# A state-space layer in fp32 on one core: D times x moved to ScalarE, decays issued earlier, the z projection ordered bank by bank

## The chip, the cores and the metric

One core of a Trainium2 chip runs the whole program. Time is device time in microseconds (us) of one execution. The engines are named as the profile names them: PE (TensorE, matmuls), DVE (VectorE), ACT (ScalarE), POOL (GpSimd) and SP (SyncE, which issues most DMAs). L followed by a number is a line of the kernel before; line numbers above 1020 differ a little in the kernel after.

## What is computed

Two request groups, a prompt of 256 tokens and eight samples of 16 tokens, 384 tokens in all, go through two layers of width 1024. The first layer is a short convolution beside forgetting attention, the second a Mamba-2 mixer; a gated convolutional FFN follows each. Everything is fp32. The change is in the second mixer, which is, cut to what matters:

```
def odd_mixer(h, conv_state, ssm_state, w_in, conv_w, conv_b, dt_bias, a_log, d_skip, norm_w, w_out):
    proj = h @ w_in
    z, xbc, dt_raw = jnp.split(proj, [D_INNER, D_INNER + CONV_DIM], axis=-1)
    xbc, new_conv = causal_dwconv(xbc, conv_state, conv_w, conv_b)
    xbc = jax.nn.silu(xbc)
    xs, bm, cm = jnp.split(xbc, [D_INNER, D_INNER + SSM_GROUPS * D_STATE], axis=-1)
    dt = jax.nn.softplus(dt_raw.astype(f32) + dt_bias.astype(f32))
    a = -jnp.exp(a_log.astype(f32))
    ...
    y, h_last = ssd_scan(xs, dt, a, bm, cm, ssm_state, chunk)
    y = y + d_skip.astype(f32)[:, None] * xs.astype(f32)
    y = y.reshape(b, length, D_INNER) * jax.nn.silu(z.astype(f32))
    y = rms_norm(y.reshape(b, length, SSM_GROUPS, D_INNER // SSM_GROUPS), ...)
    out = y.astype(h.dtype) @ w_out
```

There are four groups of eight heads, 64 wide each, so a group is 512 of the 2048 inner channels. Inside a group the scan is done by matrices: decay factors between tokens times C·B ("mix") times x gives the part within a block, the incoming state gives the part between blocks, and the states are carried on.

## The kernel before

Each large product is three matmuls (function three, L418 on): the weights and the activations are split into a high and a low part, and high times high, high times low and low times high are summed. A weight tile is 128 x 1024. It comes by one DMA of 512 KB into raw, ACT copies it to wh (L306) and DVE subtracts to get wl (L300). Three buffers each of raw, wh and wl exist; Weights.take (L385) makes the next tile ahead at high priority as soon as the current one is first used. Weights of the output projection also carry the norm's gain; such a tile is made in four pieces on ACT and four on DVE. The order in which tiles come is fixed on the host by the list that the diff's first piece changes.

In this layer PE keeps the program order (keep, L220 on); the order on the other engines comes from the Tile scheduler, which follows the program and the priorities, the work marked high priority first. PSUM is split into three banks "mm" (for the channel products xbc, the z projection and the output projection op) and five "aux" banks for all else. A bank is written again only after its reader has emptied it.

One group g goes like this:

- conv_bc and conv_x project channels: B and C are one product each of 24 matmuls of 128 x 384, and x is four products. After each product, DVE copies it to pad (times the row norm R), three DVE instructions and one of ACT do the convolution c, ACT applies silu to xf, B or C.
- turn_x (L1006) transposes the four x tiles on PE and ACT copies them to xt. Group.take (L1051) makes xdt on DVE and xw on POOL. Group.skip (L1067) makes y = D·x, on POOL, three instructions of 128 x 512, and loads the samples' states h0.
- decays (L1019) loads four tiles td from a DRAM copy of the running sums, ACT does relu in 16 instructions and exp in four (with table loads between), and Group (L1037) multiplies td by C·B on DVE.
- within (L1079) runs on PE: S, the prompt block's own state, and y from mix and xdt; inter (L1103) is yi, the part from the incoming state, for which ACT copies S to S0; states (L1119) is hn, the samples' new states, in two halves.
- project_z (L1132) is 72 matmuls of 128 x 512 into three banks (z0, z1, z2, one for each 128 tokens), from four weight tiles; Gate multiplies y by silu(z), takes the squares, builds the norm's factor rg by a chain of small DVE instructions (rqi to rqo) and turns y for the output projection add_out (L1193), which is 96 matmuls of 128 x 384 for a group, each of its eight outputs (op) added into X by DVE.

The main loop (L1264 to L1303) runs groups 0 to 2 and places within(g), yi, the next group's channel products, hn, z(g) and half or all of op(g-1) in that order. The last group (L1305 to L1321) has the same steps without new channel products. sgS is a single product ahead of the loop whose exponential decS gives the samples' decays. In the rows of the trace, tiles carry a running number that differs between the two kernels (y__5139, td__4920).

The lines around the first group, before:

```
    ps = paux("sgS")
    T.matmul(ps, lhsT=C("Us"), rhs=tjd.rearrange("p h j -> p (h j)"), start=True, stop=True)
    act(decS, ps, AF.Exp)

    decs = decays(0)
    grp = Group(0, decs, bc_)
    Bn, Cn = conv_bc(0, 1), conv_bc(1, 1)
    nx = [conv_x(1, 0)]
    grp.take(turn_x(xs))
    grp.skip()
    xs = [*nx, conv_x(1, 1)]
```

## Time and profile before

| | |
|---|---|
| median of 3 runs | 1072.57 us (1071.39 to 1074.22) |
| the profiled execution | 1072.5 us, of which the traced span is 1070.5 |
| PE busy | 1039.9 us, 97% of the span |
| DVE busy | 747.5 us, 70% |
| ACT busy | 503.9 us, 47% |
| POOL busy | 133.6 us, 12% |

The state-space mixer is on PE from about 466 to 790 us of the span. The attention layer with its FFN stands before it, the second FFN behind it. Shares of busy time are means over the whole span. What PE waits for in the mixer's stretch, and which engine is full there, is read from that stretch alone.

### The profile page before, as it was taken

The page shows a single profiled execution, that of the slowest core. Times are in us where ns is not written, and L with a number is a line of the kernel's source. Part 1 is how long each engine was busy: PE and PEld are TensorE (multiplying, and loading weights), DVE is VectorE, ACT ScalarE, POOL GpSimd, SP SyncE. Part 2 cuts the span into 40 slices and gives each one's busy share as a digit, 9 for nine tenths or more (in the row PEclk, how much of TensorE's full clock was granted, in tenths as well). Part 3 has the DMA queues.
Part 4 walks back from the last instruction along what each step waited for, and adds up shares of the span by engine and source line. Part 5 has one row for each costly group of instructions (what it writes and reads, how often), then busy time and mean ns, then how long its engine had stood idle before and what let it go on. Part 6 is the DMA issues. An engine that isn't in the chain of part 4 may idle for free.

```text
span 1070.5 us, 16702 instructions
## 1 busy us (share of the span) xinstructions
PE 1039.9 (97%) x6316; PEld 968.5 (90%) x6316; DVE 747.5 (70%) x1361; ACT 503.9 (47%) x825; POOL 133.6 (12%) x351
## 2 busy tenths in 40 slices
PE   9999999999999999999699999899999999999998
PEld 7788799999999999988577877797999999999998
DVE  7968566777776634467898978977997776765332
ACT  6344335444444433347666755663554444443221
POOL 0030010100000000013433223320001000000000
PEclk9999999999999999998899999999999999999999
DMA  8442434443434444436446463643534434344441
GB/s 286 156 148 76 159 120 125 126 131 121 135 119 136 128 128 128 125 104 189 127 137 214 144 235 128 208 144 105 178 121 127 134 120 136 119 131 140 138 148 43
DMA packets 50328, 150.30 MB, mean 140 GB/s; under 512 B 5992, under 2 KB 8312, under 8 KB 50248
## 3 DMA queue, kind: packets, MB, share of 16 engines
q1 hardware_dynamic: 44360, 136.78, 41.0%
q10 hardware_dynamic: 4608, 8.39, 2.1%
q0 software_dynamic: 1280, 4.06, 1.1%
q8 instruction: 50, 0.82, 0.3%
q14 instruction: 30, 0.25, 0.1%
HBM read 135.81 MB, written 13.40 MB: 139 GB/s over the span
## 4 chain that ended last, share of the span: by engine, by line
PE 34%; DVE 14%; ACT 4%; issue 2%; DMA 1%; ACTq 0%; POOL 0%; DVEq 0%
PE fd L240 9%; PE fg L240 9%; PE fa L240 8%; PE z L240 4%; DVE c L303 3%; DVE wl L300 2%; PE xbc L240 2%; DVE wl L303 1%; ACT wh L306 1%; DVE X L300 1%; PE y L240 1%; DVE pad L300 1%; DMA raw<-w 1%; PE op L240 1%; ACT L306 1%
## 5 line engine op out<-in xcount | busy, mean ns | idle before, releaser
L300 DVE TENSOR_TENSOR wl<-raw,wh 128x1024 fp32r<-128x1024 f32 (+1 forms) x205 | 252.2, 1231 | 140.4 <-ACT wh L306 139.9
L306 ACT ACTIVATE wh<-raw 128x1024 fp32r<-128x1024 f32 (+1 forms) x205 | 216.1, 1055 | 224.0 <-PE fd L240 95.0
L240 PE MATMUL fg<-Hh,wh 128*128 128x384 f32 x352 | 118.4, 336 | 1.0 <-DVE pad L300 1.0
L240 PE MATMUL fa<-Hl,wh 128*128 128x384 f32 x352 | 118.7, 337 | 0.4 <-DVE Hl L303 0.4
L240 PE MATMUL fg<-Hl,wh 128*128 128x384 f32 x352 | 118.6, 337 | 0.0
L240 PE MATMUL fa<-Hh,wl 128*128 128x384 f32 x352 | 118.4, 336 | 0.0
L240 PE MATMUL fg<-Hh,wl 128*128 128x384 f32 x352 | 118.4, 336 | 0.0
L240 PE MATMUL fa<-Hh,wh 128*128 128x384 f32 x352 | 118.3, 336 | 0.0
L240 PE MATMUL fd<-hh,wh 128*128 128x384 f32 x352 | 118.3, 336 | 0.0
L240 PE MATMUL fd<-hh,wl 128*128 128x384 f32 x352 | 118.3, 336 | 0.0
L240 PE MATMUL fd<-hl,wh 128*128 128x384 f32 x352 | 118.3, 336 | 0.0
L303 DVE SCALAR_TENSOR_TENSOR c<-pad,prm,c 128x400 f32<-128x400 f32 (+1 forms) x160 | 104.8, 658 | 7.0 <-ACT c L306 5.3
L240 PE MATMUL xbc<-Hh,wh 128*128 128x384 f32 x192 | 67.6, 352 | 2.1 <-DVE X L300 2.1
L240 PEld LDWEIGHTS fg<-Hh,wh 128*128 128x128 f32 x352 | 66.2, 188 | 1.3 <-ACT R L306 1.3
L240 PEld LDWEIGHTS fa<-Hl,wh 128*128 128x128 f32 x352 | 66.2, 188 | 1.0 <-DVE Hl L303 0.8
L240 PEld LDWEIGHTS fa<-Hh,wl 128*128 128x128 f32 x352 | 66.2, 188 | 0.1
L240 PEld LDWEIGHTS fg<-Hh,wl 128*128 128x128 f32 x352 | 66.2, 188 | 0.1
L240 PEld LDWEIGHTS fg<-Hl,wh 128*128 128x128 f32 x352 | 66.2, 188 | 0.1
L240 PEld LDWEIGHTS fa<-Hh,wh 128*128 128x128 f32 x352 | 66.2, 188 | 0.1
L240 PEld LDWEIGHTS fd<-hl,wh 128*128 128x128 f32 x352 | 66.2, 188 | 0.0
L240 PEld LDWEIGHTS fd<-hh,wh 128*128 128x128 f32 x352 | 66.2, 188 | 0.0
L240 PEld LDWEIGHTS fd<-hh,wl 128*128 128x128 f32 x352 | 66.2, 188 | 0.0
(803 smaller groups left out, 2140.6 us busy)
## 6 DMA issues: line engine op xcount, KB each, us to landing
raw<-w SPq DMA_DIRECT2D x219, 512.0 KB, 3.5
kc<-kc SPq DMA_DIRECT2D x8, 256.0 KB, 3.6
vc<-vc SPq DMA_DIRECT2D x8, 256.0 KB, 3.1
X<-x SPq DMA_DIRECT2D x8, 192.0 KB, 3.8
o_y<-X SPq DMA_DIRECT2D x8, 192.0 KB, 2.7
o_v<-vt POOLq DMA_DIRECT2D x3, 256.0 KB, 2.5
o_k<-kraw POOLq DMA_DIRECT2D x3, 256.0 KB, 2.6
cst<-cst SPq DMA_DIRECT2D x1, 617.0 KB, 4.8
```

The lines of the kernel that those rows point to most:

```text
L240: ins = nc.tensor.matmul(*a, **kw)
L300: (eng or V).tensor_tensor(out=out, in0=a, in1=b, op=op)
L303: V.scalar_tensor_tensor(out=out, in0=a, scalar=s, in1=b, op0=op0, op1=op1)
L306: S.activation(out, a, f, **kw)
```

## The change

- **D·x.** Three POOL instructions for each group become eight ACT instructions (Copy with a scale by head, 128 x 3 x 64 each) into one y tile for three blocks, two buffers. The late output projection's scratch o takes a buffer of xdt instead of one of y.
- **First decays.** decays is a generator in two parts: the DMAs of td first, the ACT work later. For group 0 the DMAs are issued ahead of the products bc(0,1), bc(1,1) and x(1,0), which now stand ahead of sgS; then turn_x, the ACT part of the decays, Group, take, and x(1,1) and x(1,2) stand ahead of the first y.
- **S0** is copied at high priority.
- **z.** Instead of pairs of weight tiles with banks 0 and 1 and then bank 2, project_z takes half of the contraction (four takes, two weight tiles) and runs it bank by bank, 12 matmuls each. In group 0 a third of z now stands ahead of hn's first half, a third between the halves, and a third behind.
- **Output half.** In group 2, 48 matmuls of op stand behind the last channel product and ahead of hn's second half and the third z; the weights' order and the gain positions follow.

```diff
--- before.py
+++ after.py
@@ -132,7 +132,7 @@

     bc(0, 0), bc(1, 0), xs(0), bc(0, 1), bc(1, 1), xs(1), tm(wi, 0)
     bc(0, 2), bc(1, 2), xs(2, (0, 1)), out(0, (0, 256)), xs(2, (2, 3)), tm(wi, 512), out(0, (512, 768))
-    bc(0, 3), bc(1, 3), xs(3), tm(wi, 1024), out(1), tm(wi, 1536), out(2), out(3)
+    bc(0, 3), bc(1, 3), xs(3), out(1, (0, 256)), tm(wi, 1024), out(1, (512, 768)), tm(wi, 1536), out(2), out(3)
     ffn(1)
     w = np.concatenate(blocks, 1)
     a["w"] = w.reshape(P, -1, RC).transpose(1, 0, 2)
@@ -353,7 +353,7 @@
             self.tiles, self.made, self.raw, self.pos = {}, 0, None, 0

             t, self.gain = 32 + 3 * NF + 8, {}
-            for g, at in enumerate(((12, 13, 20, 21), range(32, 36), range(40, 44), range(44, 48))):
+            for g, at in enumerate(((12, 13, 20, 21), (28, 29, 34, 35), range(40, 44), range(44, 48))):
                 self.gain.update({t + i: 4 * g for i in at})
             self.total = d["w"].shape[0] * (RC // WC)

@@ -1021,13 +1021,16 @@
         out = []
         for b in range(2):
             for hf in range(2):
-                c0 = 8 * g + 4 * hf
                 dec = t512("td", 4, (P, 4, P))
-                nc.sync.dma_start(out=dec, in_=rows[b, c0:c0 + 4, :].partition_broadcast(P))
+                nc.sync.dma_start(out=dec, in_=rows[b, 8 * g + 4 * hf:8 * g + 4 * hf + 4, :].partition_broadcast(P))
+                out.append(dec)
+        yield
+        for b in range(2):
+            for hf in range(2):
+                c0, dec = 8 * g + 4 * hf, out[2 * b + hf]

                 for i in range(4):
                     act(dec[:, i, :], dec[:, i, :], AF.Relu, scale=-1.0, bias=cumK[:, 32 * b + c0 + i:32 * b + c0 + i + 1])
-                out.append(dec)
         for dec in out:
             act(dec, dec, AF.Exp, scale=-1.0)
         return out
@@ -1071,10 +1074,11 @@
                 h0 = t512("h0", 8)
                 nc.sync.dma_start(out=h0, in_=d["h0"][bb, self.g])
                 self.h0.append(h0)
-            for b in range(3):
-                y = t512("y", 6)
-                tt(heads(y[:, :]), heads(self.xt[:, b, :]), bc64(prr("dsk", 32)[:, self.h8]), ALU.mult, G)
-                self.ys.append(y)
+            y = t512("y", 2, (P, 3, 512))
+            for h in range(8):
+                o = slice(64 * h, 64 * h + 64)
+                act(y[:, :, o], self.xt[:, :, o], AF.Copy, scale=prc("dsk", 8 * self.g + h))
+            self.ys = [y[:, b, :] for b in range(3)]

         def within(self):

@@ -1085,7 +1089,8 @@
                     T.matmul(ph, lhsT=self.Bt[:, b, :], rhs=self.xw[b], start=True, stop=True)
                     if b == 0:
                         self.S0 = t512("S0", 1)
-                        act(self.S0, ph, AF.Copy)
+                        with tc.high_priority():
+                            act(self.S0, ph, AF.Copy)
                     else:
                         S1 = self.xt[:, 0, :]
                         tt(heads(S1), heads(self.S0[:, :]), bc64(E[:, 224 + 8 * g:232 + 8 * g]), ALU.mult)
@@ -1132,14 +1137,13 @@
     def project_z():

         ps = [pmm(f"z{b}") for b in range(3)]
-        for k0 in range(0, KT, 2):
-            ws = [W.take(512) for _ in range(2)]
-            for bs in ((0, 1), (2,)):
+        for k0 in (0, 4):
+            ws = [W.take(512) for _ in range(4)]
+            for b in range(3):
+                o = slice(b * P, (b + 1) * P)
                 for i, (wh, wl) in enumerate(ws):
-                    for b in bs:
-                        o = slice(b * P, (b + 1) * P)
-                        three(ps[b], Hh[:, k0 + i, o], Hl[:, k0 + i, o], wh, wl, k0 + i == 0, k0 + i == KT - 1)
-                        yield
+                    three(ps[b], Hh[:, k0 + i, o], Hl[:, k0 + i, o], wh, wl, k0 + i == 0, k0 + i == KT - 1)
+                    yield
         zs = t512("zs", 1, (P, 3, 512))
         for b in range(3):
             act(zs[:, b, :], ps[b], AF.Silu, scale=r[:, b:b + 1])
@@ -1203,7 +1207,7 @@
                 if factor is None:
                     residual(m0 + m, ps)
                 else:
-                    o = t512("y", 6, (P, NT))
+                    o = t512("xdt", 3, (P, NT))
                     tt(o, ps[:, :NT], factor, ALU.mult)
                     tt(X[:, m0 + m, :], X[:, m0 + m, :], o, ALU.add)
                     norm_tile(m0 + m, "g_ffn", 1, o1)
@@ -1246,6 +1250,10 @@
     cumK = o0.tile([P, 64], F32, name="cumK")
     V.tensor_copy(cumK, ps[:, 0:64])
     tt(wdt, E[:, 96:192], dt, ALU.mult)
+    decs = decays(0)
+    next(decs)
+    Bn, Cn = conv_bc(0, 1), conv_bc(1, 1)
+    nx = [conv_x(1, 0)]
     tjd = t512("h0", 8, (P, 32, LB))
     tt(tjd, dA[:, 64:96].unsqueeze(2).broadcast_to([P, 32, LB]),
        C("Tj").unsqueeze(1).broadcast_to([P, 32, LB]), ALU.mult)
@@ -1253,13 +1261,11 @@
     T.matmul(ps, lhsT=C("Us"), rhs=tjd.rearrange("p h j -> p (h j)"), start=True, stop=True)
     act(decS, ps, AF.Exp)

-    decs = decays(0)
-    grp = Group(0, decs, bc_)
-    Bn, Cn = conv_bc(0, 1), conv_bc(1, 1)
-    nx = [conv_x(1, 0)]
-    grp.take(turn_x(xs))
+    xt = turn_x(xs)
+    grp = Group(0, run(decs), bc_)
+    grp.take(xt)
+    xs = [*nx, conv_x(1, 1), conv_x(1, 2)]
     grp.skip()
-    xs = [*nx, conv_x(1, 1)]
     op = gate = None
     for g in range(4):
         last = g == 3
@@ -1271,20 +1277,24 @@
             op = add_out(*gate.y2, None)
         if last:
             break
-        decs = decays(g + 1)
+        decs = run(decays(g + 1))
         xs.append(conv_x(g + 1, len(xs)))
         grp.inter(1)
         bc_ = turn_bc(g + 1, Bn, Cn)
-        if g == 1:
+        z = project_z()
+        if g == 0:
+            steps(z, 8)
+        elif g == 1:
             steps(op, 16)
         else:
-            xs.append(conv_x(g + 1, len(xs)))
+            xs.append(conv_x(3, 1))
         grp.states(0)
-        z = project_z()
         if g == 0:
-            steps(z, 12)
+            steps(z, 8)
         while len(xs) < 4:
             xs.append(conv_x(g + 1, len(xs)))
+        if g == 2:
+            steps(op, 16)
         grp.states(1)
         nxt = Group(g + 1, decs, bc_)
         zs = steps(z)
```

In the following lists, one row is one instruction, or a run of equal ones (x4), in the order of its engine's stream.

ACT, first group, ahead of the first y. Before, from the first exponential of td to the copy of S (td__4920 is what the first y needs; xt is the transposed x; wh are weight tiles for later products):

```order
L306 ACTIVATE td__4920<-td__4920 128x512
L306 ACTIVATE wh_5297<-raw_5295 128x1024
L306 ACTIVATE td__4926<-td__4926 128x512
L306 ACTIVATE td__4932<-td__4932 128x512
L306 ACTIVATE td__4938<-td__4938 128x512
L306 ACTIVATE c4_4993<-pad4_4986,prm_74 128x408
L306 ACTIVATE c4_5039<-pad4_5032,prm_74 128x408
L306 ACTIVATE xt__5092<-xT_5093 128x512
L306 ACTIVATE xt__5092<-xT_5099 128x512
L306 ACTIVATE xt__5092<-xT_5105 128x512
L306 ACTIVATE wh_5365<-raw_5363 128x1024
L306 ACTIVATE S0__5193<-S_5191 128x512
```

After, the same stretch up to the first exponential of td (td__4915 is now what the first y needs):

```order
L306 ACTIVATE wh_5346<-raw_5344 128x1024
L306 ACTIVATE td__4919<-td__4919,cumK_4912 128x128 x4
L306 ACTIVATE td__4921<-td__4921,cumK_4912 128x128 x3
L306 ACT_TABLE_LOAD
L306 ACTIVATE xf__5015<-c4_5054 128x256
L306 ACTIVATE wh_5415<-raw_5413 128x1024
L306 ACTIVATE S0__5242<-S_5240 128x512
L306 ACTIVATE xf__5015<-c4_5054 128x128
L306 ACTIVATE td__4921<-td__4921,cumK_4912 128x128
L306 ACT_TABLE_LOAD
L306 ACTIVATE td__4915<-td__4915 128x512
```

The exponentials, which stood ahead of xt and of S0, now stand behind S0 and a second table load, with two weight copies ahead of them.

DVE, first group. Before, ending with the first xdt (c4 and pad4 are convolutions, xdt__5111 the operand of the first y):

```order
L303 SCALAR_TENSOR_TENSOR c4_4993<-pad4_4986,prm_74,c4_4993 128x408
L303 SCALAR_TENSOR_TENSOR c4_5039<-pad4_5032,prm_74,c4_5039 128x408
L303 SCALAR_TENSOR_TENSOR c4_4993<-pad4_4986,prm_74,c4_4993 128x408
L303 SCALAR_TENSOR_TENSOR c4_5039<-pad4_5032,prm_74,c4_5039 128x408
L303 SCALAR_TENSOR_TENSOR c4_4993<-pad4_4986,prm_74,c4_4993 128x408
L300 TENSOR_TENSOR wl_5366<-raw_5363,wh_5365 128x1024
L303 SCALAR_TENSOR_TENSOR c4_5039<-pad4_5032,prm_74,c4_5039 128x408
L300 TENSOR_TENSOR pad4_5078<-xbc_5047,R_79 128x256
L300 TENSOR_TENSOR pad4_5078<-xbc_5047,R_79 128x8x16
L300 TENSOR_TENSOR xdt__5111<-xt__5092,dt_4535 128x512
L300 TENSOR_TENSOR xdt__5115<-xt__5092,dt_4535 128x512
L303 SCALAR_TENSOR_TENSOR c4_5085<-pad4_5078,prm_74,c4_5085 128x408
```

After, ending with the four td:

```order
L300 TENSOR_TENSOR wl_5347<-raw_5344,wh_5346 128x1024
L303 SCALAR_TENSOR_TENSOR c4_5054<-pad4_5047,prm_74,c4_5054 128x408
L300 TENSOR_TENSOR xdt__5119<-xt__5066,dt_4535 128x512
L300 TENSOR_TENSOR pad4_5155<-xbc_5124,R_79 128x256
L300 TENSOR_TENSOR pad4_5155<-xbc_5124,R_79 128x8x16
L300 TENSOR_TENSOR pad4_5201<-xbc_5170,R_79 128x256
L300 TENSOR_TENSOR pad4_5201<-xbc_5170,R_79 128x8x16
L300 TENSOR_TENSOR wl_5416<-raw_5413,wh_5415 128x1024
L300 TENSOR_TENSOR td__4915<-td__4915,CB__4833 128x512
L300 TENSOR_TENSOR td__4917<-td__4917,CB__4833 128x512
L300 TENSOR_TENSOR td__4919<-td__4919,CB__4833 128x512
L300 TENSOR_TENSOR td__4921<-td__4921,CB__4833 128x512
```

xdt stood behind two products' convolutions. Now it stands ahead of the pads of the next ones, and td comes last, behind a weight tile's wl.

DVE, group 2, around the start of the third z. Before (pad4_6891 empties the bank of the last channel product, h0 are the samples' states, wl_7009 is the first gain tile):

```order
L300 TENSOR_TENSOR pad4_6891<-xbc_6860,R_79 128x256
L303 SCALAR_TENSOR_TENSOR c4_6852<-pad4_6845,prm_74,c4_6852 128x408
L300 TENSOR_TENSOR pad4_6891<-xbc_6860,R_79 128x8x16
L300 TENSOR_TENSOR h0__6536<-h0__6536,hn_6905 128x512
L300 TENSOR_TENSOR h0__6540<-h0__6540,hn_6906 128x512
L303 SCALAR_TENSOR_TENSOR c4_6898<-pad4_6891,prm_74,c4_6898 128x408
L300 TENSOR_TENSOR h0__6544<-h0__6544,hn_6907 128x512
L303 SCALAR_TENSOR_TENSOR c4_6898<-pad4_6891,prm_74,c4_6898 128x408
L300 TENSOR_TENSOR h0__6548<-h0__6548,hn_6908 128x512
L303 SCALAR_TENSOR_TENSOR c4_6898<-pad4_6891,prm_74,c4_6898 128x408
L300 TENSOR_TENSOR wl_6985<-raw_6982,wh_6984 128x1024
L303 SCALAR_TENSOR_TENSOR wl_7009<-raw_7006,prm_74,wh_7008 128x256 x4
```

After (op_6932 is the first output of the op half; X is the residual):

```order
L300 TENSOR_TENSOR mix__7017<-CB__6742,decS_4539 128x1024
L300 TENSOR_TENSOR wl_6963<-raw_6960,wh_6962 128x1024
L303 SCALAR_TENSOR_TENSOR c4_6861<-pad4_6854,prm_74,c4_6861 128x408
L303 SCALAR_TENSOR_TENSOR c4_6913<-pad4_6906,prm_74,c4_6913 128x408
L303 SCALAR_TENSOR_TENSOR c4_6861<-pad4_6854,prm_74,c4_6861 128x408
L303 SCALAR_TENSOR_TENSOR c4_6913<-pad4_6906,prm_74,c4_6913 128x408
L300 TENSOR_TENSOR wl_7025<-raw_7022,wh_7024 128x1024
L303 SCALAR_TENSOR_TENSOR c4_6861<-pad4_6854,prm_74,c4_6861 128x408
L303 SCALAR_TENSOR_TENSOR c4_6913<-pad4_6906,prm_74,c4_6913 128x408
L300 TENSOR_TENSOR X_73<-X_73,op_6932 128x384
L300 TENSOR_TENSOR X_73<-X_73,op_6946 128x384
L300 TENSOR_TENSOR X_73<-X_73,op_6966 128x384
```

The convolutions of the last two x products and two wl now stand ahead of the first addition that empties an op bank, and the gain tiles have moved further up, out of these rows.

## Rows read from the trace of the kernel before

**Rows 1.** What PE waited for between 466 and 805 us, by what it waited for: us in total, times, longest.

```profile
PE y L240 <- DVE xdt__5111 L300: 7.9, 1, 7.9
PE z L240 <- DVE pad L300: 3.7, 2, 3.4
PE sgS L240 <- DVE h__4915 L300: 2.4, 1, 2.4
PE xbc L240 <- DVE X L300: 1.4, 1, 1.4
PE yi L240 <- ACT S__5785 L306: 1.3, 1, 1.3
```

**Rows 2.** Windows of all engines: from:to, length, busy us (instructions) of PE, PEld, DVE, ACT and POOL, granted TensorE clock, DMA share, GB/s.

```profile
490.00:500.00 10.00, 7.56 (x34) 5.67 (x33) 8.88 (x17) 9.78 (x14) 4.17 (x9) 0.76 0.59 185
500.00:510.00 10.00, 10.00 (x54) 10.00 (x53) 3.33 (x6) 6.58 (x19) 0.78 (x4) 0.90 0.87 272
...
520.00:530.00 10.00, 2.95 (x34) 2.32 (x34) 10.00 (x13) 3.06 (x6) 8.07 (x12) 0.63 0.22 67
...
656.70:694.90 38.20, 34.62 (x243) 28.08 (x242) 37.59 (x62) 26.26 (x53) 14.70 (x21) 0.96 0.58 190
```

**Rows 3.** Timeline of PE around the first group: start us, us, engine, line, operation, out<-in, count, and in brackets the wait before it.

```profile
495.82 2.07 PE L240 MATMUL sgS<-h__4915,cst 128*128 128x512 f32 x2 [2.44 <-DVE h__4915 L300]
...
512.17 0.27 PE L245 MATMUL xT<-cst,xf__4691 128*128 128x128 f32 x1
...
518.04 1.13 PE L240 MATMUL S<-xw__5113,Bt__4840 128*128 128x512 f32 x2 [0.22 <-POOL xw__5113 L300]
...
527.05 0.38 PE L240 MATMUL y<-xdt__5111,td__4920 128*64 128x64 f32 x2 [7.88 <-DVE xdt__5111 L300]
```

**Rows 4.** Timeline of PE, second group: the start of its first channel product and of what follows 72 matmuls later.

```profile
567.03 0.42 PE L240 MATMUL xbc<-Hh,wh 128*128 128x384 f32 x1
...
579.61 1.02 PE L240 MATMUL S<-xw__5613,Bt__5354 128*128 128x512 f32 x2
```

**Rows 5.** Timeline of ACT, first group: one td tile's relu, the table load behind it, the first exponential.

```profile
509.30 1.26 ACT L306 ACTIVATE td__4938<-td__4938,cumK 128x128 f32<-128x128 f32 x4
510.59 1.28 ACT L306 ACT_TABLE_LOAD   x1
511.88 0.63 ACT L306 ACTIVATE td__4920<-td__4920 128x512 f32<-128x512 f32 x1
```

**Rows 6.** Timeline of DVE, first group, up to the operand of the first y.

```profile
516.45 6.00 DVE L303 SCALAR_TENSOR_TENSOR c<-pad,prm,c 128x408 f32<-128x408 f32 x5
522.37 2.06 DVE L300 TENSOR_TENSOR wl<-raw,wh 128x1024 fp32r<-128x1024 f32 x1
...
526.23 0.68 DVE L300 TENSOR_TENSOR xdt__5111<-xt__5092,dt 128x512 f32<-128x512 f32 x1
```

**Rows 7.** Windows with the instructions of tile z alone (columns as in Rows 2, engines that have none left out): the two halves of the first z, then the second and the third z whole.

```profile
547.00:556.20 9.20, 8.82 (x36) 6.61 (x36) 0.00 (x0) 1.00 0.45 153
557.30:565.80 8.50, 8.50 (x36) 6.68 (x36) 1.38 (x2) 1.00 0.96 308
...
616.00:633.50 17.50, 17.18 (x72) 13.36 (x72) 1.38 (x2) 1.00 0.81 277
683.80:705.70 21.90, 18.48 (x72) 14.37 (x72) 1.38 (x2) 0.92 0.82 268
```

**Rows 8.** Timeline of ACT: a weight copy in the first z, and the last gain copies and the copy of S in group 1.

```profile
562.15 1.06 ACT L306 ACTIVATE wh<-raw 128x1024 fp32r<-128x1024 f32 x1 [4.75 <-DMA raw<-w]
...
583.83 1.69 ACT L306 ACTIVATE wh<-raw,prm 128x256 fp32r<-128x256 f32 x4
585.42 0.57 ACT L306 ACTIVATE S__5785<-S 128x512 f32<-128x512 f32 x1
```

**Rows 9.** Timeline of POOL, group 1: one D·x.

```profile
572.84 1.56 POOL L300 TENSOR_TENSOR y__5779<-xt__5565,prm 128x512 f32<-128x512 f32 x1
```

**Rows 10.** Timeline of DVE, group 1: two instructions of the chain to rg, of 128 x 3 elements each.

```profile
571.93 0.97 DVE L311 TENSOR_SCALAR rqi<-v 128x3 int32<-128x3 int32 x1
...
575.46 0.16 DVE L303 SCALAR_TENSOR_TENSOR rqb<-rqa,v 128x3 f32<-128x3 f32 x1
```

**Rows 11.** Timeline of PE: half of op(0) and two channel products (to S of group 2), and the whole op(1) (to S of group 3).

```profile
634.72 0.42 PE L240 MATMUL op<-yh,wh 128*128 128x384 f32 x1
...
654.03 1.02 PE L240 MATMUL S<-xw__6357,Bt__5973 128*128 128x512 f32 x2
...
706.91 0.42 PE L240 MATMUL op<-yh,wh 128*128 128x384 f32 x1
...
724.23 0.59 PE L240 MATMUL S<-xw__7097,Bt__6740 128*128 128x512 f32 x1
```

**Rows 12.** Timeline of DVE, group 2: the pads of x(3,0), then later a convolution step, a wl, a gain tile's wl, and an addition into X.

```profile
668.75 0.61 DVE L300 TENSOR_TENSOR pad<-xbc,R 128x256 f32<-128x256 f32 x2
...
693.56 0.64 DVE L303 SCALAR_TENSOR_TENSOR c<-pad,prm,c 128x408 f32<-128x408 f32 x1
694.32 1.23 DVE L300 TENSOR_TENSOR wl<-raw,wh 128x1024 fp32r<-128x1024 f32 x1
698.02 1.68 DVE L303 SCALAR_TENSOR_TENSOR wl<-raw,prm,wh 128x256 fp32r<-128x256 f32 x4 [2.48 <-ACT wh L306]
...
709.90 0.55 DVE L300 TENSOR_TENSOR X<-X,op 128x384 f32<-128x384 f32 x1
```

## The prediction

> **What bounds the kernel now.** PE is busy for 97% of the span, so only PE's stream counts: where it waits, and where its clock is down. I read the waits of PE in the mixer's stretch first [rows 1]. There are 16.7 us in five of them: the first y (7.9), the third z (3.4 of 3.7), sgS (2.4), the products behind the first op half (1.4) and the second group's yi (1.3). The windows come next [rows 2]. The granted clock is 0.76, 0.90 and 0.63 in the windows in and behind the waits of sgS and y, where PE stood idle, so PE runs part of them at the lower of its two levels, and a wait removed can give back more than its own length. Third is what ends each wait: PE's timeline [rows 3], then ACT [rows 5] and DVE [rows 6] behind it. The reader is to see that the first y waits for DVE, which at that point works off two products' convolutions, and that DVE is full around the third z (37.59 of 38.2 us) [rows 2]. The sum is made against the profiled execution, 1072.5 us, 0.07 below the median.
>
> **sgS: -5.1.** Before, sgS starts at 495.82 after 2.44 idle, and 72 xbc matmuls later the transposes start at 512.17 [rows 3]: 16.35 us. At the full clock those 72 take 12.58 [rows 4]; the first of sgS's two passes shown as one row and their issue take about 1.06, half of that row's 2.07. So 16.35 - 13.64 = 2.7 went to the low clock. Now 72 products stand where PE waited; h__4915 is long done when PE gets to sgS. Gain 2.44 + 2.7 = 5.1. Bounds: 2.4, if the clock falls anyway, and 5.1.
>
> **First y: -3.0.** With that, sgS runs at about 506 and S of the first block starts at about 517, behind 24 products more than before. The y behind it needs td, and td now has a longer way on ACT: relu (1.26 a tile), a table load (1.28), xf, a weight copy (1.06), S0 (0.57), the rest of a relu, another table load, one exponential (0.63), then DVE's product (0.68) [rows 5, 6, 8]. From S's end at 518.1: S0 to 518.9, the small ones to 519.7, the load to 521.0, the exponential to 521.6, DVE to 522.4, and about 0.6 for the weight tile's wl ahead of it: 523.0. PE waits 5 there against 8.1 (7.88 and 0.22 [rows 3]), so -3.0. Bounds: 0 (it waits 8 again: a DMA or a conv queue in front of td) and -7 (ACT gets ahead of S0). The 24 products moved ahead are work either way. The low clock behind the wait [rows 2] I keep at its cost of before.
>
> **First z: +1.5.** Bank by bank, two weight tiles must stay until bank 2 has used them. The fourth tile's buffers come free at matmul 30 of 72 and are needed at matmul 43: 13 matmuls at 8.50 / 36 = 0.236 [rows 7] cover 3.07 us. Its wh (1.06 [rows 8]) and wl (1.23 [rows 12]) take 2.3, plus about 0.4 of handing over: covered on idle engines. But DVE's queue holds mix, td and the h additions in that stretch, of which I put four (0.68 each [rows 6]) in front: 5.3 - 3.07 = 2.2 of waiting. The first half lost 0.7 before (9.2 against 8.5 [rows 7]). Net +1.5; bounds -0.7 and +4.
>
> **Second group: -2.0.** POOL's D·x ran beside DVE's small chain to rg, whose 128 x 3 instructions took 0.97 there and 0.16 beside idle POOL [rows 9, 10]; four such cost about 3.3 us of rg. The eight new ACT instructions are bounded by the 0.31 that a 128-element relu adds in a row of four (1.26 / 4) and by the 0.57 of a 128 x 512 copy [rows 5, 8]; 192 elements lie near the lower end, 0.34 each, 2.75 a group. rg therefore comes 3.3 earlier and ACT is 2.75 later: half a microsecond ahead, and S0 also passes one of four gain pieces (1.69 / 4 = 0.4 [rows 8]). That takes 0.9 of yi's 1.3 wait [rows 1]; the two waits of yT behind it lose about the same 1.1 together, since DVE's additions of y no longer stand behind the stretched chain. Bounds -2.4 and +1 (at 0.57 each, ACT is 4.6 later and S0 1.3 late).
>
> The Trainium skill, "SBUF — State Buffer", section "Who interferes with whom", says that a DVE instruction with two SBUF inputs contends with a GpSimd operation that reads SBUF, and that one of them blocks for the whole instruction. By that, all of the 1.5 us of each D·x beside DVE would come back, also under the 6.00 us of five convolution steps; the trace agrees as far as two-input steps go, but rqi, with one input, was slow as well. Taking it whole would give the larger gain that is the first rival below.
>
> Speaking against the change, the Trainium skill, "ScalarE: Activation LUTs", section "Rules for kernel authors", wants multiplications on VectorE and not on ScalarE. By the costs in its section "What ACT_TABLE_LOAD costs", an estimate for 192 elements with one pointer operand is 0.35 us back to back, 2.8 a group. No row here has this form; 2.8 would leave the sum as it is.
>
> **Second z: +0.4.** The same tile boundary with a less loaded DVE: I take 0.9 of waiting, less the 0.5 that this z loses now (17.5 against 2 x 8.5 [rows 7]). Bounds -0.5 and +3.
>
> **First op half: -2.2.** From op to S it takes 19.31 us [rows 11]. Full-clock pieces give 48 op at 17.32 / 96 [rows 11] = 8.66 and 48 xbc at 12.58 x 48 / 72 [rows 4] = 8.39, together 17.05. The missing 2.2 are X additions late on a DVE that POOL held up, the 1.4 of [rows 1] among them. I take it all back; bounds 0 and -2.3.
>
> **Third z and the new op half: +1.6.** Before, this z lost 21.9 - 17.0 = 4.9 [rows 7]: 3.4 of waiting for the last pad, which empties the third bank, and 1.5 of clock. Now 48 op stand between. Three banks: the fourth output needs the first X addition, which stands on DVE behind all convolutions. From the pads at 668.75 [rows 12] to it there are 12 convolution steps (0.64), 3 wl (1.23), 2 gain tiles (1.68), 12 additions and td (0.68), mix (as a wl, 1.23), 4 pads (0.61), CB (0.6) and the addition (0.55) [rows 6, 12]: 27.7, less 0.08 of overlap at each of some 40 [rows 6]: 24.5. That is 693.5 to 694, where PE wants the bank at about 682.8 + 36 x 0.18 = 689.3. So 4.5 to 5 of waiting, and 1.5 of clock behind it: 6.5 against 4.9. Bounds: +4, and -4.5 where DVE, rid of POOL, is early.
>
> **The rest: 0.** The fourth z, the late add_out's scratch, and the DMA issues of decays on SP, moved ahead of three products whose raw loads they precede by four issues, are covered by PE's work. Bounds 0 and +0.5.
>
> Sum: -5.1 - 3.0 + 1.5 - 2.0 + 0.4 - 2.2 + 1.6 = -8.8, so 1063.7 us.
>
> **The rivals.**
> *DVE is freed further.* If each of four groups loses some 4.5 us of POOL's D·x beside DVE (3 x 1.5 [rows 9]), the backlog in front of the third z is gone: no boundary waits in the z's (first -0.7, second -0.5) and -4.5 at the third: -5.1 - 3.0 - 0.7 - 2.4 - 0.5 - 2.2 - 4.5 = -18.4, 1054 us; I take 1056, as the chain of convolutions itself stays. For it: rqi's 0.97 against 0.16 for its like. Against it: DVE is paced by products that come no faster.
> *The first y waits as before.* The way over ACT has two table loads; one more weight copy or a late DMA keeps 8: the sum is -5.8, and with boundary waits of 1 us more, 1067.7. Against it: the row sum ends 4 us early.
> *The z's starve: slower.* Every half boundary has to wait for a tile whose raw comes late; one weight copy waited 4.75 us for its DMA [rows 8], beside a DMA share of 0.96 [rows 7]. If in all four z the fourth tile is ready 3.5 us late, with 1.5 of clock behind it, that is 20, against 12.3 of other gains: 1080 us. It decides from the point where raw lands less than 2.7 us before matmul 43. Against it: three raws are held ahead.
> *DVE paces all.* It is 37.59 of 38.2 full [rows 2]; if PE's gains are only waited for later, the time stays at 1071. Against it: the waits of sgS and the first y lie ahead of that stretch, and windows behind the third z are not full.
>
> **How the numbers follow.** Chances: forecast 0.53 (1060 to 1067), DVE freed 0.15, first y as before 0.15, DVE paces all 0.09, starving 0.08. The range leaves out the last two: 1054.5 to 1069. A measurement tells 0.3% (3.2 us): faster is below 1069.4, which holds the first three, but for 0.02 of the third: 0.81; same: 0.09 + 0.02 = 0.11; slower 0.08.
>
> **What would show it.** In the profile after: no wait of sgS and a clock of 1.0 there; a first y at about 523 with a wait near 5, released by td; in the first z one wait of about 2 at its middle, by a wl; small DVE instructions of 0.16 throughout; an op in group 2 that waits 4 to 5 for X. A first y at 527 or later, waits at several half boundaries, or no wait at op's fourth output would make the sum wrong at that term.

## The result and the profile after

The changed kernel took 1062.71 us (median of 4 runs, 1061.36 to 1065.19) against 1072.91 (1071.39 to 1074.22) before: a ratio of 0.9908, 95% interval 0.9885 to 0.9931. On a second chip it was 1063.06 against 1069.46, 0.9931 (0.9914 to 0.9948). The forecast, 1063.7, is 0.9918 of the 1072.5 us it was summed against. The profiled execution of after is the slowest of its four, 1065.19 us with a span of 1063.4.

The same view as [rows 1], what PE waited for in the mixer, of the changed kernel:

```profile
PE y L240 <- DVE td__4915 L300: 4.6, 1, 4.6
PE op L240 <- DVE X L300: 3.8, 1, 3.8
PE z L240 <- DVE wl L300: 1.6, 2, 0.9
PE z L240 <- ACT wh L306: 1.0, 2, 0.7
...
PE z L240 <- DVE pad L300: 0.5, 1, 0.5
PE op L240 <- DVE pad L300: 0.5, 1, 0.5
```

The waits of sgS, of yi and of the third z are gone. The first y still waits, now for td; two waits are new, in the z's (wl and wh) and at op's fourth output (X). The windows of all engines that answer to [rows 2]:

```profile
490.00:500.00 10.00, 10.00 (x64) 9.50 (x63) 8.71 (x19) 7.65 (x11) 3.69 (x8) 1.00 0.53 155
500.00:510.00 10.00, 10.00 (x61) 9.47 (x60) 8.34 (x15) 8.17 (x18) 3.12 (x13) 1.00 0.90 312
...
520.00:530.00 10.00, 7.29 (x114) 4.62 (x114) 8.45 (x15) 9.95 (x21) 2.34 (x7) 0.83 0.48 150
...
680.00:690.00 10.00, 8.25 (x34) 5.75 (x35) 6.37 (x12) 2.23 (x5) 0.00 (x0) 0.83 0.37 106
```

The granted clock is 1.00 where it was 0.76 and 0.90; it is down only in the windows of the two long waits that are left. PE's timeline around the first group, to be read beside [rows 3]:

```profile
506.56 0.59 PE L240 MATMUL sgS<-h__5061,cst 128*128 128x512 f32 x1
...
507.42 0.27 PE L245 MATMUL xT<-cst,xf__4691 128*128 128x128 f32 x1
...
517.06 0.59 PE L240 MATMUL S<-xw__5113,Bt__4840 128*128 128x512 f32 x1
...
522.71 0.34 PE L240 MATMUL y<-xdt__5111,td__4915 128*64 128x64 f32 x2 [4.63 <-DVE td__4915 L300]
```

The stages on PE, in us from one first matmul to the next, in two profiles of each kernel ("again" is e9 and e1 below; "term" is the prediction's). Stages that are equal are left out.

| stage | before | after | before, again | after, again | change by pair | term |
|---|---|---|---|---|---|---|
| first xbc to the transposes | 52.12 | 46.51 | 51.66 | 46.51 | -5.6, -5.2 | -5.1 |
| to the first y, 24 xbc (4.17) more | 14.88 | 15.29 | 14.88 | 15.29 | -3.8, -3.8 | -3.0 |
| to the first z, 24 xbc and a hn (1.07) less | 20.02 | 13.62 | 19.84 | 14.92 | -1.2, +0.3 | 0 |
| first z, a hn more | 18.72 | 21.16 | 18.90 | 21.04 | +1.4, +1.1 | +1.5 |
| S of group 1 to the second z | 36.39 | 34.38 | 36.39 | 34.39 | -2.0, -2.0 | -2.0 |
| second z | 17.49 | 18.87 | 17.49 | 18.87 | +1.4, +1.4 | +0.4 |
| transposes, op half, two products | 20.54 | 18.06 | 19.26 | 18.09 | -2.5, -1.2 | -2.2 |
| S of group 2 to S of group 3 | 70.20 | 70.73 | 70.17 | 72.43 | +0.5, +2.3 | +1.6 |
| second FFN's up projections | 186.82 | 190.26 | 186.75 | 186.99 | +3.4, +0.2 | 0 |

From the first xbc to the FFN the mixer gained 11.7 us in the first pair and 7.1 in the second; the forecast of 8.8 lies between. Each is a difference of two single executions, the second pair's on two chips. The FFN's 3.4 has a section below.

### The profile page after: what moved, and what is told of

Read it like the earlier page. It is cut to its first block, busy times and chain, and to the rows that moved or that the text cites. A ratio compares the mean times of both kernels' runs of the same rounds, so it can differ in the third digit from the quotient of the medians.

```text
span 1063.4 us, 16718 instructions
## 1 busy us (share of the span) xinstructions
PE 1039.9 (98%) x6316; PEld 969.7 (91%) x6316; DVE 739.8 (70%) x1361; ACT 511.6 (48%) x855; POOL 104.4 (10%) x339
## 4 chain that ended last, share of the span: by engine, by line
PE 38%; DVE 13%; ACT 3%; issue 2%; DMA 0%; ACTq 0%; DVEq 0%
PE fg L240 9%; PE fd L240 9%; PE fa L240 8%; PE z L240 4%; PE xbc L240 3%; DVE wl L300 2%; DVE c L303 2%; PE op L240 2%; DVE wl L303 1%; DVE X L300 1%; ACT wh L306 1%; PE y L240 1%; DVE pad L300 1%; PE S L240 0%; ACT L306 0%
## 5 line engine op out<-in xcount | busy, mean ns | idle before, releaser
L303 DVE SCALAR_TENSOR_TENSOR c<-pad,prm,c 128x400 f32<-128x400 f32 (+1 forms) x160 | 101.9, 645 | 7.9 <-ACT c L306 6.2
```

The lines of the kernel that those rows point to most:

```text
L303: V.scalar_tensor_tensor(out=out, in0=a, scalar=s, in1=b, op0=op0, op1=op1)
```

## The experiments

All ratios are against the kernel before on the same chip. The runs came from four chips: e1, e2, e4 and e5; e3, e7, e8 and e9; e6, e11 and e12; e13. The kernel before had medians of 1069.46, 1070.42, 1070.17 and 1069.82 us there. The changed kernel was run only on the first of them (e1) and on the chip of the result, so a difference of e6, e7, e8, e11, e12 or e13 from e1's 1063.06 is one across chips and uncertain by about 1 us more than its runs spread.

| run | median us | ratio, 95% interval |
|---|---|---|
| e1 changed kernel again | 1063.06 | 0.9931 (0.9914 to 0.9948) |
| e2 changed, D·x on POOL | 1069.49 | 0.9998 (0.9987 to 1.0008) |
| e3 before, D·x on ACT alone | 1062.24 | 0.9927 (0.9905 to 0.9949) |
| e4 before, first decays alone | 1063.83 | 0.9938 (0.9922 to 0.9953) |
| e5 changed, old order in z | 1059.85 | 0.9903 (0.9886 to 0.9920) |
| e6 changed, no op half | 1057.80 | 0.9872 (0.9857 to 0.9887) |
| e7 changed, additions into X first | 1058.12 | 0.9889 (0.9866 to 0.9912) |
| e8 e5 and e7 together | 1053.72 | 0.9847 (0.9825 to 0.9868) |
| e9 kernel before again | 1072.15 | a single execution |
| e11 changed, D·x on DVE | 1064.97 | 0.9947 (0.9932 to 0.9962) |
| e12 e8, one more product first | 1051.61 | 0.9824 (0.9809 to 0.9840) |
| e13 changed, o_hs from POOL | 1056.65 | 0.9878 (0.9858 to 0.9898) |

**e1 and e9, both kernels again.** No edit.

> The changed kernel once more, nothing edited. Its first profiled execution was 1065.2 us, the slowest of four (1061.4 to 1065.2), and its second FFN's fa and fg matmuls followed each other at 0.174 and 0.179 us in turn where the kernel before has 0.173 throughout, 3.3 us in all. If that rhythm is a chance of the execution, this profile shows 0.173 there at about 1061.5 to 1063 us. The rival is that the change causes it: then 0.174 and 0.179 stand there again and the profiled span is again 3.8 us over what the mixer's gain gives.

The FFN ran at 0.173 a step and was 187.0 us long, so its rhythm is not the change's. But the profiled execution took 1064.9 and not the 1061.5 to 1063 expected: what the FFN did not lose, the mixer did. The waits are the first profile's (y 4.6, op for X 3.8), and the windows behind them differ in the clock. Windows of all engines of e1:

```profile
520.00:530.00 10.00, 7.19 (x102) 5.49 (x106) 7.66 (x14) 9.94 (x22) 2.43 (x7) 0.66 0.40 133
...
680.00:690.00 10.00, 6.41 (x21) 4.51 (x22) 5.22 (x10) 2.23 (x5) 0.09 (x1) 0.66 0.40 136
```

0.66 stands where the first profile has 0.83. By these two figures, an estimate, each such window does 1.7 us less of full-clock work in its 10 us; the stages to the first z and to S of group 3 are 1.3 and 1.7 longer. So the low clock behind one and the same wait cost different times in these two executions.

> The kernel before once more, nothing edited, for its stages on the chip of these runs: on the chip of the runs of e1 to e5 its median was 1069.5 us, 3 us under its first chip's 1072.6, while the changed kernel stood at 1063.1 on both. If the 3 us are the time that the low clock lasts behind its waits (as the two profiles of the changed kernel differ, 1.3 and 1.7 us behind equal waits), the waits here are the first profile's (y 7.9, z 3.4, sgS 2.4) and the granted clock behind them is higher in some window. Rival: the waits themselves differ, by 1 us or more in sum.

The waits were y 7.9, z 3.9 and sgS 2.4, the first profile's to 0.2; but this execution took 1072.15 us, above its chip's median of 1070.42, so it can't show where 3 us went. That stays open.

**e2, D·x back on POOL.**

```diff
-            y = t512("y", 2, (P, 3, 512))
-            for h in range(8):
-                o = slice(64 * h, 64 * h + 64)
-                act(y[:, :, o], self.xt[:, :, o], AF.Copy, scale=prc("dsk", 8 * self.g + h))
-            self.ys = [y[:, b, :] for b in range(3)]
+            for b in range(3):
+                y = t512("y", 6)
+                tt(heads(y[:, :]), heads(self.xt[:, b, :]), bc64(prr("dsk", 32)[:, self.h8]), ALU.mult, G)
+                self.ys.append(y)
```

> The changed kernel with D times x back on POOL, three instructions of 128 x 512 a group, all else as changed. Theory (POOL held up DVE's small chain to rg and the X additions): the gain of group 1 (2.8 us from S to op) and of the first op half (2.5 us) is lost, so 5 us above the changed kernel, 1067 to 1068 us; the small DVE instructions take 1.0 us again in group 1. Rival (those gains come from the copy of S0 at high priority and from an earlier group 0): within 1 us of the changed kernel, 1062 to 1064 us. A second rival is that the eight ACT instructions cost as much as they give: below 1062 us.

All the other edits together bring nothing: 0.9998. The loss, 6.4 us, is 1.4 more than expected, and only a part of it lies where it was expected. S of group 1 to op takes 15.77 us, against 14.33 in the changed kernel and 17.10 before: two of the four small DVE instructions take 1.01 again, the other two stay at 0.16 to 0.17. The stage of the first op half is 18.64 against 18.06, so it loses 0.6 and not 2.5. The largest loss was not expected: the first y waits 7.1 us instead of 4.6. Group 3's yi waits 1.2, which it does not in the changed kernel. ACT's timeline in e2 and then in the changed kernel shows what delays the first y:

```profile
514.59 1.28 ACT L306 ACT_TABLE_LOAD   x1
518.69 0.42 ACT L306 ACTIVATE xf__5015<-c 128x256 f32<-128x256 f32 x1 [2.82 <-DVE c L303]
...
522.34 0.63 ACT L306 ACTIVATE td__4915<-td__4915 128x512 f32<-128x512 f32 x1
```

```profile
516.05 1.28 ACT L306 ACT_TABLE_LOAD   x1
517.65 0.42 ACT L306 ACTIVATE xf__5015<-c 128x256 f32<-128x256 f32 x1 [0.32 <-DVE c L303]
...
520.01 1.28 ACT L306 ACT_TABLE_LOAD   x1
521.30 0.63 ACT L306 ACTIVATE td__4915<-td__4915 128x512 f32<-128x512 f32 x1
```

xf stands ahead of td's exponential and waits for a convolution on DVE, 2.8 us in the one and 0.3 in the other. In e2's DVE timeline the steps in front of it are stretched; beside it, POOL's timeline with xw and D·x (tile y):

```profile
513.25 1.42 DVE L303 SCALAR_TENSOR_TENSOR c<-pad,prm,c 128x408 f32<-128x408 f32 x1
514.59 1.53 DVE L300 TENSOR_TENSOR xdt__5115<-xt__5066,dt 128x512 f32<-128x512 f32 x1
516.04 2.06 DVE L300 TENSOR_TENSOR wl<-raw,wh 128x1024 fp32r<-128x1024 f32 x1
```

```profile
512.74 1.49 POOL L300 TENSOR_TENSOR xw__5117<-xt__5066,wdt 128x512 f32<-128x512 f32 x1
514.19 1.38 POOL L300 TENSOR_TENSOR y__5233<-xt__5066,prm 128x512 f32<-128x512 f32 x1
515.53 1.49 POOL L300 TENSOR_TENSOR y__5235<-xt__5066,prm 128x512 f32<-128x512 f32 x1
```

The same three in the changed kernel, where POOL has only xw and is through earlier:

```profile
514.70 0.63 DVE L303 SCALAR_TENSOR_TENSOR c<-pad,prm,c 128x408 f32<-128x408 f32 x1
515.25 0.68 DVE L300 TENSOR_TENSOR xdt__5115<-xt__5066,dt 128x512 f32<-128x512 f32 x1
515.86 1.21 DVE L300 TENSOR_TENSOR wl<-raw,wh 128x1024 fp32r<-128x1024 f32 x1
```

A c and an xdt ahead of these, beside POOL's xw, still take 1.49 and 1.53 there.

**e3, D·x on ACT alone** (e2's edit the other way, in the kernel before, with the scratch o moved).

> The kernel before with only D times x moved to ACT (and the scratch o in a buffer of xdt). Theory (POOL's D times x beside DVE costs some 6 us, in four places: the first y, group 1 from S to op, the first op half, and the last z): small DVE instructions of 0.16 in group 1, the first y's wait shorter by 2 to 4 us, and 4 to 7 us under the kernel before. Rival (the first y waits for td on ACT or for the c chain itself, and without the early decays ACT has no room): within 2 us of the kernel before.

8.2 us under the kernel before, as much as the whole change and above the 4 to 7 expected. The first y waits 5.5 instead of 7.9, S of group 1 to the second z is 34.60 with no wait of yi left, and the chain to rg has rqi at 0.17.

**e11, D·x on DVE.** The three products of e2's new lines run on DVE, into the changed kernel's y tile.

> The changed kernel with D times x on DVE instead of ACT, three instructions of 128 x 512 a group. It tells whether the gain of that part comes from POOL no longer running beside DVE, or from ACT having room. Theory (POOL beside DVE was the cost, 6 us in all): DVE pays 3 x 0.68 = 2.0 us a group, of which the full stretches (groups 0 to 2) pass on about half, so 1 to 4 us above the changed kernel, 1064 to 1067 us, under the 1069.5 of D times x on POOL. Rival (any 2 us on DVE cost as much as POOL did): 1068 us or more.

1.9 us above the changed kernel by the medians, though the two ratios' intervals overlap, and clearly under D·x on POOL (0.9947 against 0.9998). DVE can carry D·x itself for less than POOL's running beside it costs; whether ACT is better still, these runs don't tell. That most of the gain is the removal of D·x from POOL, and not room on ACT, is shown by this together with e2.

**e4, the first decays alone**, in the kernel before (the generator in decays and its calls in the loop are as in the change; the diff leaves them out).

```diff
...
+    decs = decays(0)
+    next(decs)
+    Bn, Cn = conv_bc(0, 1), conv_bc(1, 1)
+    nx = [conv_x(1, 0)]
     tjd = t512("h0", 8, (P, 32, LB))
...
-    decs = decays(0)
-    grp = Group(0, decs, bc_)
-    Bn, Cn = conv_bc(0, 1), conv_bc(1, 1)
-    nx = [conv_x(1, 0)]
-    grp.take(turn_x(xs))
+    xt = turn_x(xs)
+    grp = Group(0, run(decs), bc_)
+    grp.take(xt)
+    xs = [*nx, conv_x(1, 1), conv_x(1, 2)]
     grp.skip()
-    xs = [*nx, conv_x(1, 1)]
...
```

> The kernel before with only the first decays' part of the change: DMAs of td early, the products of group 1 ahead of sgS, the ACT part behind, x(1,1) and x(1,2) ahead of the first y. Theory (sgS 5.6 and the first y 3.8 to 4.9 us, kept to the end): 1062 to 1063.5 us, nearly all of the whole change's gain, since the other parts add to about 0. Rival (DVE paces all from group 1 on, so that time gained before is waited for later): 1067 us or more.

The time, 1063.83, is 0.3 us above the theory's range and far from the rival's, but the parts are not the theory's: sgS gives its 5.2 to 5.6 us (46.51 to the transposes), while the first y waits 6.6 for td and gives only 1.8 us of the 3.8. xf waits 2.82 for c here as in e2, so the rest of that term belongs to D·x. The gain is not given back later: from the transposes of group 1 to the second z both are 50.20 long, and DVE does not pace the rest.

**e5, the old order inside z.**

```diff
-        for k0 in (0, 4):
-            ws = [W.take(512) for _ in range(4)]
-            for b in range(3):
-                o = slice(b * P, (b + 1) * P)
-                for i, (wh, wl) in enumerate(ws):
+        for k0 in range(0, KT, 2):
+            ws = [W.take(512) for _ in range(2)]
+            for bs in ((0, 1), (2,)):
+                for i, (wh, wl) in enumerate(ws):
+                    for b in bs:
+                        o = slice(b * P, (b + 1) * P)
...
```

> The changed kernel with the z projection's old inner order (pairs of weight tiles, banks 0 and 1 and then 2), its placing in the groups as changed. Theory (the half boundary waits for the fourth tile's conversion, 1.4 us in the first z and 1.4 in the second): both waits go, 1.5 to 2.8 us faster than the changed kernel, 1060 to 1061 us. Rival: the third bank is needed 12 instead of 24 matmuls into z, so that it waits for pads or X additions instead: 1063 us or more, with a wait of z for DVE pad or X of 1 us or more.

3.2 us faster than the changed kernel, more than expected. The first z takes 19.43 instead of 21.04 to 21.16, the second 16.91 instead of 18.87, and no wait for wl or wh is left. Some of it is given back: S of group 1 to the second z is 35.75 instead of 34.39, with two new waits of yT for DVE's y, 1.7 us in all. The boundary in the changed kernel, PE's timeline in the first and in the second z, 43 matmuls in:

```profile
547.97 0.50 PE L240 MATMUL z<-wh,Hh 128*128 128x512 f32 x1 [0.31 <-ACT wh L306]
549.36 0.50 PE L240 MATMUL z<-wl,Hh 128*128 128x512 f32 x1 [0.89 <-DVE wl L300]
...
616.43 0.50 PE L240 MATMUL z<-wh,Hh 128*128 128x512 f32 x1 [0.71 <-ACT wh L306]
617.69 0.50 PE L240 MATMUL z<-wl,Hh 128*128 128x512 f32 x1 [0.76 <-DVE wl L300]
```

**e13, the stores of the samples' states issued from POOL.**

```diff
-                nc.scalar.dma_start(out=d["o_hs"][bb, self.g], in_=h0)
+                nc.gpsimd.dma_start(out=d["o_hs"][bb, self.g], in_=h0)
```

> The changed kernel with the stores of the samples' states (o_hs) issued from POOL instead of ACT. In the changed kernel the fourth weight tile's wh in the first z stands on ACT behind three such issues, which wait for DVE's additions (ACT idle 2.2 us, ended by h), and PE waits 0.3 us for that wh and then 0.9 for its wl; the second z waits 0.7 and 0.8. Theory (DVE's queue sets it: mix and an h addition stand ahead of that wl in any case, and in the second z wh stands behind a silu that waits for DVE's c): PE's waits in the two z's keep their sum of 2.7 us within 1 us, and the time stays within 1.5 us of the changed kernel, 1061.5 to 1064.5. Rival (ACT, held by the issues, sets it): the waits for wh and wl in the first z go, 1060 to 1061.5 us. POOL's issuing may also hold up DVE again: then above 1064.5 us.

The first z stayed at 21.03 us: ACT's wh came earlier, and PE waited 1.34 for wl alone, behind mix and an addition into h on DVE. The waits for wh and wl in the two z's sum to 2.1, so that part of the theory holds. The forecast of the time was wrong: 1056.65 is 6.4 us under the changed kernel. The scheduler also put DVE's work of group 2 into another order, the first addition into X ahead of mix and of a wl; the fourth op waited 1.2 instead of 3.8, and S of group 2 to S of group 3 took 66.82 instead of 70.73 and 72.43.

This bears on every run here. An edit that touches no product and no DVE instruction moved the time by as much as D·x did, and 3.9 to 5.6 us of it lie in the stage where the scheduler gave DVE another order. A difference between two of these kernels is therefore the edit and the new order together; the waits and stages beside it tell which part is likely to be the edit's own.

**e7, the additions into X at high priority.**

```diff
-                    residual(m0 + m, ps)
+                    with tc.high_priority():
+                        residual(m0 + m, ps)
```

> The changed kernel with the additions of op into X marked high priority, all else as changed; DVE's order then has the first of them ahead of six of the convolution steps and one wl that stood in front. Theory (the fourth op waits because X stands behind those steps): the wait of 3.8 us for X falls to 1 us or less, and with some low clock behind it the time falls by 3 to 5 us, 1058 to 1060 us. Rival (DVE is simply late there, so what is moved behind makes the third z wait instead): the wait moves to z, pad or y, and the time stays within 1 us, 1062 to 1064.

As the theory had it, 4.9 us faster by the medians: the wait for X is gone, and the window 680 to 690 runs at a clock of 1.00.

```profile
680.00:690.00 10.00, 10.00 (x48) 7.36 (x46) 7.15 (x13) 3.36 (x6) 0.00 (x0) 1.00 0.69 244
```

S of group 2 to S of group 3 is 65.2 us instead of 70.7 and 72.4. The second z lost more here (21.66 instead of 18.87, with 2.4 us of waits instead of 1.5, and a granted clock of 0.87 in the window 610 to 620), so something of the order moved there too.

**e6, no op half ahead of the third z.**

```diff
-    bc(0, 3), bc(1, 3), xs(3), out(1, (0, 256)), tm(wi, 1024), out(1, (512, 768)), tm(wi, 1536), out(2), out(3)
+    bc(0, 3), bc(1, 3), xs(3), tm(wi, 1024), out(1), tm(wi, 1536), out(2), out(3)
...
-        if g == 2:
-            steps(op, 16)
         grp.states(1)
```

> The changed kernel without its new place for half of op(1): 96 matmuls of op behind the third z as before, weights in the old order, all else as changed. Theory (from the stages: S of group 2 to S of group 3 takes 70.2 us in the kernel before, 70.7 in the changed one): the third z waits 3.4 us for the last pad again, the fourth op no longer 3.8 us for X, and the time is within 1.5 us of the changed kernel, 1061.5 to 1064.5 us. Rival (the half does cover the pads, and the X wait is cheaper than the pad wait): 1065 us or more.

5.3 us faster than the changed kernel by the medians, which neither theory nor rival had; S of group 2 to S of group 3 takes 67.79 us instead of 70.73 and 72.43. Bank by bank, the third z asks for its third bank 12 matmuls later, and the pad is all but there: it waits 0.4 us for it and not 3.4. What PE waited for in e6:

```profile
PE z L240 <- DVE wl L300: 2.4, 3, 0.9
PE z L240 <- ACT wh L306: 2.3, 3, 1.5
...
PE z L240 <- DVE pad L300: 0.9, 2, 0.5
```

The same wait in e3 and then in e4, which have the old order in z and no op half in front of it:

```profile
PE z L240 <- DVE pad L300: 3.8, 2, 3.1
```

```profile
PE z L240 <- DVE pad L300: 3.4, 1, 3.4
```

So neither D·x nor the first decays by itself takes that wait away. The third z now has its own boundary wait, without a low clock, and takes 20.30 (72 matmuls) where it took 21.84 before the change. The op half therefore guarded against a wait that the new order in z had all but removed, and brought the wait for X instead.

**e8 and e12, towards a faster kernel.** e8 is e5 and e7 together. e12 is e8 with x(1,3) ahead of the first y (its edit against e8):

```diff
-    xs = [*nx, conv_x(1, 1), conv_x(1, 2)]
+    xs = [*nx, conv_x(1, 1), conv_x(1, 2), conv_x(1, 3)]
...
-        xs.append(conv_x(g + 1, len(xs)))
+        if g:
+            xs.append(conv_x(g + 1, len(xs)))
         grp.inter(1)
```

> Both edits: the old order inside z (e5, 1059.9 us) and the additions into X at high priority (e7). Theory (two waits in different places, each with its own late instruction): their gains add, 1055 to 1057 us. Rival (with pairs, z's third bank needs the X additions earlier, so that the two overlap): 1058 us or more.

> The best kernel so far (e8: old order in z, X additions at high priority, 1053.7 us) with one more product, x(1,3), ahead of the first y. Theory (the first y waits 4.6 us for td, which comes over ACT and not behind the products): the 24 matmuls of 4.2 us fill the wait, it falls to 1 us or less, the low clock behind it goes too, and the time is 1047 to 1050 us. Rival (ACT's and DVE's order follows the program, so the fourth product's convolution and weight tile push td back by as much): the wait stays above 2 us, 1052 us or more.

e8's gains add: 9.3 us below the changed kernel, against 3.2 and 4.9 alone. e12 removes the first y's wait (0.9 is left, at a later td), but by the medians it gains 2.1 and not 4 to 6, and the intervals of e8 and e12 overlap. Two waits take its place:

```profile
PE xbc L240 <- ACT zs__5555 L306: 2.5, 1, 2.5
PE z L240 <- DVE pad L300: 1.9, 1, 1.9
...
PE y L240 <- DVE td__4919 L300: 0.9, 1, 0.9
```

The products behind the first z now wait until ACT has emptied its banks. At 1051.6 us it is well under both kernels.

## Why the prediction was right

The time and its sign came out by the sum, and every stage of the mixer lies within 1.2 us of its term in both pairs. The main mechanisms are the ones reckoned: work standing where PE waited, and D·x gone from beside DVE. That the sum met the median to 1 us is partly luck: terms missed by up to 1.2 us, some one way and some the other, and single executions differ by 4. Point by point:

- **sgS, -5.1:** -5.2 and -5.6. 72 products stand in the wait, and the low clock behind it went with it, as reckoned; e4 shows the same with that part alone.
- **First y, -3.0:** the y came with a wait of 4.63 where I had 5, so -3.8. The way over ACT is the one I counted: table load, xf, wh, S0, relu, table load, exponential. The 0.6 us put in for a wl ahead of td did not come (DVE stood idle for 1.55 before td). And the step "xf" was taken as free of waiting, which holds only without POOL's D·x: e2 waits 7.1, e4 6.6. About half of the term is D·x's and not the new order's; the attribution failed and the size held.
- **First z, +1.5:** +1.1 to +1.4, at the tile and the matmul named, with DVE's mix and h in front of wl (e13, e5). Both parts were smaller than reckoned: the boundary cost 1.6 to 1.7 (the stage against e5's 19.43) and not 2.2, and 0.4 to 0.5 of the old loss came back and not 0.7.
- **Second group, -2.0:** -2.0 in both pairs. By parts: eight D·x took 1.83 and 1.14 us, 2.97 a group against my 2.75, and rqi 0.15. ACT's timeline in group 1, then DVE's:

```profile
562.31 1.83 ACT L306 ACTIVATE y__5780<-xt__5568,prm 128x192 f32<-128x192 f32 x5
...
566.52 1.14 ACT L306 ACTIVATE y__5780<-xt__5568,prm 128x192 f32<-128x192 f32 x3
...
574.45 0.58 ACT L306 ACTIVATE S__5791<-S 128x512 f32<-128x512 f32 x1
```

```profile
564.30 0.15 DVE L311 TENSOR_SCALAR rqi<-v 128x3 int32<-128x3 int32 x1
...
568.49 0.15 DVE L303 SCALAR_TENSOR_TENSOR rg<-rqb,rqo 128x3 f32<-128x3 f32 x1
```

  S's copy comes 3.15 us behind S (571.30) instead of 5.81, more than the 0.9 I had, and both yT waits are gone with yi's. D·x alone brings this stage to 34.60 (e3). The copy of S at high priority has no run of its own; in e2, which has it with D·x on POOL, group 1's yi does not wait either and the stage is 35.97, so most of the term is D·x's.
- **Second z, +0.4:** +1.4. This term was mis-sized: 0.9 of waiting was taken, 1.5 came, because here wh stands behind a silu on ACT (xf) that waits for DVE's c.
- **First op half, -2.2:** -2.5 and -1.2; the kernel before itself varied by 1.3 in this stage. The size held, the reason did not: I had POOL's D·x hold up the additions into X, but with D·x back on POOL (e2) the stage is 18.64, only 0.6 longer than in the changed kernel. With D·x alone (e3) it is 18.99, with the first decays alone (e4) 19.66. What brings the rest is not shown.
- **Third z and op half, +1.6:** +0.5 and +2.3. The count of DVE's queue held: from the pads to the first addition into X I had 24.5 us, the trace has 25.0. But 668.75 and 24.5 make 693.25 and not 693.5 to 694, which is 4.0 us behind 689.3; PE waited 3.8, so the rows were right and the 4.5 to 5 was a slip in adding up. With 4.0 the term is +0.6 by its own rows. DVE's timeline, group 2:

```profile
656.15 0.61 DVE L300 TENSOR_TENSOR pad<-xbc,R 128x256 f32<-128x256 f32 x2
...
676.69 2.29 DVE L303 SCALAR_TENSOR_TENSOR c<-pad,prm,c 128x408 f32<-128x408 f32 x4
678.91 1.22 DVE L300 TENSOR_TENSOR wl<-raw,wh 128x1024 fp32r<-128x1024 f32 x1
680.04 1.19 DVE L303 SCALAR_TENSOR_TENSOR c<-pad,prm,c 128x408 f32<-128x408 f32 x2
681.15 1.47 DVE L300 TENSOR_TENSOR X<-X,op 128x384 f32<-128x384 f32 x3
```

  What I did not ask is what the third z would do without the op half under the new order (e6).
- **The rivals.** The two of "DVE freed" and "the first y as before" did not come, though the second was nearer than I thought: without D·x's move the first y waits 7.1 (e2) and 6.6 (e4). The starving z stayed at 1 to 1.5 us a boundary, in two z's. DVE did not pace the rest: e4, e7 and e8 keep what they gain.

By parts, from medians: D·x on ACT is worth 8.2 us alone (e3) and 6.4 in the changed kernel (e2); the first decays alone 5.6 (e4). Against them stand 3.2 for the order in z (e5) and 5.3 for the op half (e6). The net of 8.8 that I forecast had the last two at 1.9 and 1.6. These worths are not terms of one sum: each is measured with another set of the other parts present, each run has its own order on DVE (e13), and no run has D·x and the first decays without the rest.

The Trainium skill, "SBUF — State Buffer", section "Who interferes with whom", says that a DVE instruction with two SBUF inputs contends with a GpSimd operation that reads SBUF, and that issue order decides which of them is blocked. The runs agree that they contend: c, xdt and wl take 1.42, 1.53 and 2.06 us beside xw and D·x on POOL and 0.63, 0.68 and 1.21 without; which of the two blocks was not tried. The same section names tensor_scalar, which is what rqi is, among the operations that can take the shared pair when their operands meet certain conditions; I had read its 0.97 as speaking against the rule. No run here tries those conditions.

The Trainium skill, "ScalarE: Activation LUTs", section "Rules for kernel authors", prefers VectorE for multiplications. Instruction for instruction the traces agree: D·x of group 1 takes 2.97 us on ACT, and three times 0.68 on DVE in e11. For the kernel's time it brought no gain here: 1063.1 us on ACT against 1065.0 on DVE, which with overlapping intervals shows neither ahead.

## What to carry to other kernels

A small job on POOL can be paid for by DVE, and then by whoever waits for DVE, as D·x was here; before it is called hidden, look for DVE rows that take twice their usual time beside it. Before a wait is filled with other work, ask whether another part of the same change has removed it already, and which buffer the filling needs: here three PSUM banks made the fourth output wait for an addition at the end of DVE's queue, and a priority on that addition was worth 4.9 us by the medians. Running a product bank by bank holds weight tiles longer, so that here, with three buffers, the fourth tile came late. And where a scheduler sets the order, a small edit can move the time in good part through a new order (e13): compare the stages before giving a gain to the edit.

## What the hardware showed that was not expected

One and the same wait cost different times in two executions: behind 4.6 and 3.8 us of waiting, the granted clock of the window was 0.83 in one and 0.66 in the other, 1.3 and 1.7 us of difference. Executions of the changed kernel spread over 4 us; these 3 are of that size.

In the first profile of the changed kernel, the up projections of the second FFN ran at steps of 0.174 and 0.179 us in turn, 3.4 us in all, at a granted clock of 1.00, and returned to 0.173 with the down projection; in e1 they ran at 0.173 throughout. Windows of all engines, the first profile and then e1:

```profile
850.00:900.00 50.00, 50.00 (x285) 50.00 (x284) 34.78 (x59) 21.91 (x31) 3.75 (x24) 1.00 0.39 122
```

```profile
850.00:900.00 50.00, 50.00 (x290) 50.00 (x290) 35.54 (x61) 22.77 (x30) 3.75 (x24) 1.00 0.42 127
```

285 matmuls against 290 in the same 50 us, of the same kernel. No other profile of this study has it. What starts and ends it was not tried and stays open.
